# Hybrid DiT trunk: the norms' factors of the time mixing spread by VectorE instead of GpSimd

## The chip, the cores and the metric

The kernel runs on one core of a Trainium2 chip. The metric is the time of one execution on the device in microseconds; the times shown are medians of several runs. A profile comes from one further execution, whose own time stands beside its span.

## The reference

Two layers of a trunk work on 256 context tokens and 256 latent tokens of width 1024. Each layer has an adaLN-modulated RMSNorm, one combined input projection that feeds three token mixers (windowed attention, bidirectional RWKV-7 time mixing, a gated spatial unit), gates that merge them, an output projection, and a dense SwiGLU. The change touches the time mixing alone, at two normalisations over the 64 columns of a head:

```python
kk = heads((k * lp['k_k']).astype(f32))
kk = kk * lax.rsqrt(jnp.sum(kk * kk, -1, keepdims=True) + 1e-12)
...
y = jnp.moveaxis(ys[:, 0] + jnp.flip(ys[:, 1], axis=0), 0, 1)
mu = jnp.mean(y, -1, keepdims=True)
var = jnp.mean(jnp.square(y - mu), -1, keepdims=True)
y = ((y - mu) * lax.rsqrt(var + GN_EPS)).reshape(B, T, C) * lp['ln_w'] + lp['ln_b']
```

The first is the norm of the keys, the second the group norm of the time mixing's output. Layer 0 needs both for all 512 tokens; layer 1, the last, needs the keys for 512 and the output for the 256 latent tokens only.

## The kernel before, in words

Activations lie feature-major: 128 features on the partitions (two heads of 64), tokens along the columns. Products of the projections are made in three passes: weights and activations are split into a high and a low part (`split`, lines 128 to 130: ScalarE casts, VectorE subtracts), and TensorE multiplies high by high, high by low and low by high (`proj`, line 92 through `dm`).

A layer has three stages. `phase_ab` holds the input projections and the three mixers, `phase_m` merges them, `phase_f` is the SwiGLU. In the profiled execution the mixers' stages lie at about 75 to 700 us (layer 0) and 1275 to 1776 us (layer 1).

`phase_ab` is written as a set of generators, one kind for each piece of work: K (`t_common`, keys, values and norm of the keys of one head pair), P (`t_prep`, the decays and scores of one stream), I (`t_inv`, a triangular inverse made on VectorE by lines 645 and 646), C (`t_chain`, the recurrence over chunks, small matmuls of lines 696 to 730, with GpSimd scaling the state in line 709), Q (`t_post`, the group norm and gate of the output), G (the gate projections), T, A and S (attention and the spatial unit, whose gelu has a GpSimd product in line 932). Start times per kind are written by hand in the table `CB` and sorted by `slots` into the order in which the generators are advanced; each kind also has a priority. From this the framework plans the order of the instructions on each engine. Every engine then runs its own list in that order and waits for semaphores.

The norms work as follows. `rnorm` (lines 418 to 430) lets TensorE sum the squares over the columns of each head with a matrix of ones (line 423), so that the sums of 128 tokens stand on the partitions, two heads side by side. `rsqrt` (lines 132 to 142) computes the inverse square root in twelve short VectorE steps (lines 136 to 142) on at most eight columns; its result is `rn`. Lines 428 and 429 spread each factor over 64 columns into the tile `rx`: a product of the repeated factor and a repeated tile of ones, 128x512, or 128x256 for the output norm of layer 1. `rnorm2` (line 436) transposes `rx` on TensorE into PSUM (`knb` for the keys, `gnb` for the output), and VectorE multiplies it onto the keys (line 508) or the output (line 754). `rx` shares a ring of three buffers, `tmp`, with other temporary tiles. There are four head pairs in each layer, each with one norm of the keys and one of the output: 16 calls of `rnorm` in all.

Of the kernel before, what the change touches and what calls it, by code (L numbers as in the profile page):

```python
# [85 lines left out]
def trunk(ctx: ExitStack, tc: tile.TileContext, out, a):  # L86
# [11 lines left out]
    V = nc.vector  # L98
    S = nc.scalar
    G = nc.gpsimd  # L100
# [31 lines left out]
    def rsqrt(pool, out, x, scale, bias, tag):  # L132

        xs = pool.tile(list(out.shape), F32, tag=tag + "x", bufs=1, name="rsx")
        t = pool.tile(list(out.shape), F32, tag=tag + "t", bufs=1, name="rst")
        V.tensor_scalar(xs, x, scale * RS_A, bias * RS_A, op0=ALU.mult, op1=ALU.add)
        V.tensor_scalar(t.bitcast(I32), xs.bitcast(I32), 1, 0x7fffffff, op0=ALU.logical_shift_right, op1=ALU.bitwise_xor)
        V.tensor_scalar(out, t, RS_B, None, op0=ALU.mult)
        for _ in range(3):
            V.tensor_mul(t, out, out)  # L140
            V.scalar_tensor_tensor(t, t, -0.5 / RS_A, xs, op0=ALU.mult, op1=ALU.mult)
            V.scalar_tensor_tensor(out, t, 1.5, out, op0=ALU.add, op1=ALU.mult)
# [234 lines left out]
    def phase_ab(L, extra):  # L377
# [7 lines left out]
        with tc.tile_pool(name="pb", bufs=1, reuse_waits="tile", side="right") as pb, tc.tile_pool(name="pe", bufs=1, reuse_waits="tile") as pe, tc.tile_pool(name="pbp", bufs=1, space=PSUM, reuse_waits="tile") as pbp:  # L385
# [4 lines left out]
            def rc(shape, name):  # L390
                return pbp.tile(shape, F32, tag="rc", bufs=cb["PB"]["rc"], name=name) if "rc" in cb["PB"] else rw(shape, name)
# [4 lines left out]
            def tmc(name, n=512):  # L396
                return pb.tile([128, n], F32, tag="tmc", bufs=cb["BF"]["tmc"], name=name) if "tmc" in cb["BF"] else tmp(name, n)
# [20 lines left out]
            def rnorm(sq, n, scale, bias, name):  # L418

                nt = n // 128  # L420
                pss = rc([128, 4, 2], name + "s")
                for j in range(nt):
                    mm(pss[:, j], sq[:, 128 * j:128 * j + 128], bones[:, 0:128:64], start=True, stop=True)
                rn = pb.tile([128, 4, 2], F32, tag="rn", bufs=2, name="rn")
                rsqrt(pb, rn[:, :nt], pss[:, :nt], scale, bias, "rr")
                rx = tmc("rx")
                rxv = rx[:, :n].rearrange("p (a h d) -> p a h d", h=2, d=64)
                G.tensor_tensor(rxv, rn[:, :nt].unsqueeze(3).broadcast_to([128, nt, 2, 64]),
                                ones[:, 0:64].unsqueeze(1).unsqueeze(1).broadcast_to([128, nt, 2, 64]), op=ALU.mult)
                return rx  # L430

# [42 lines left out]
            def t_common(hp):  # L474
# [26 lines left out]
                sq = tmc("sqk")  # L501
                S.activation(sq, kT, AF.Square, scale=kkc)
                rx = rnorm(sq, 512, 1.0, 1e-12, "kn")
                yield
                rn = rnorm2(rx, 512, "kn")
# [235 lines left out]
            def t_post(hp):  # L741

                need("C", 2 * hp + 1, 99)
                h = H[hp]
                y = h.y
                pm = rc([128, 512], "pm")
                mm(pm[:, :no], bones, y, start=True, stop=True)
                V.scalar_tensor_tensor(y, pm[:, :no], -1.0 / 64, y, op0=ALU.mult, op1=ALU.add)
                sq = tmc("sqy")
                S.activation(sq[:, :no], y, AF.Square)  # L750
                yield
                rx = rnorm(sq, no, 1.0 / 64, 64e-5, "gn")
                yield
                V.tensor_mul(y, y, rnorm2(rx, no, "gn"))
                V.tensor_scalar(y, y, pv[:, V_LW + hp:V_LW + hp + 1], pv[:, V_LB + hp:V_LB + hp + 1], op0=ALU.mult, op1=ALU.add)
                need("K", hp, 99)
                G.tensor_add(y, y, h.bv)
                yield
                pg = rc([128, 512], "pg")
                mm(pg[:, :no], L.gup[:, 128 * hp:128 * hp + 128], sxg, start=True, stop=True)  # L760
                V.tensor_mul(y, y, pg[:, :no])
                G.dma_start(orw_d[:, hp, 256 * so:512], y)
                yield
# [495 lines left out]
```

## Time and profile before

| what | value |
|---|---|
| median of 3 runs | 2076.11 us (2067.94 to 2082.16) |
| profiled execution, its own time | 2055.66 us |
| its span, first to last instruction | 2053.9 us |
| mean granted clock of TensorE | 0.943 |
| busy: TensorE | 1913.0 us |
| busy: VectorE | 1355.0 us |
| busy: ScalarE | 854.5 us |
| busy: GpSimd | 237.7 us |
| instructions | 35061 |

Busy times of the engines lie beside each other and do not add up to the span. A view of waits gives the idle time of an engine ahead of an instruction and the instruction that ended it. The chain that ended last is followed back from the last instruction, at each step to what released it. A granted clock of 1.00 is TensorE's higher level, 2.4 GHz; 0.50 is the lower, 1.2 GHz; a value between them is a mean over a stretch.

### The profile page before, as it was taken

To read this page: it belongs to the slowest core of one execution; us is meant where nothing else is said; L and a number is where in the kernel's file an instruction comes from. 1 tells how busy PE (TensorE), PEld (TensorE's weight loads), DVE (VectorE), ACT (ScalarE), POOL (GpSimd) and SP (SyncE) were. 2 spreads that over 40 slices of the span, in tenths; PEclk is the share of its full clock that TensorE was granted. 3 is DMA by queue.
4 is the path that set the end of the run, shared out by engine and by line. 5 is a ranking of instruction groups with operands and counts; after the bars stand their busy time and mean duration, and the time that the engine had idled before them with its cause. 6 is when DMAs were issued, how large, how long until landed. Compare 5 with 4: busy or idle time off the path is not lost.

```text
span 2053.9 us, 35061 instructions
## 1 busy us (share of the span) xinstructions
PE 1913.0 (93%) x13162; PEld 1527.6 (74%) x13162; DVE 1355.0 (66%) x3657; ACT 854.5 (42%) x1848; POOL 237.7 (12%) x401
## 2 busy tenths in 40 slices
PE   4999989999999989899999997889998999698999
PEld 3877776666666768787887885777776777598999
DVE  4587776477585445688656545696786877476665
ACT  3442333444354433432232334444444555255443
POOL 3111201101001012100000002212020201120000
PEclk8997999989999999999999998988997999599999
DMA  8222213221211585166556422311220222374553
GB/s 286 78 67 79 63 47 114 83 90 53 63 39 55 202 269 163 62 188 212 176 175 212 145 79 76 100 66 32 93 69 14 74 75 88 122 230 146 185 183 105
DMA packets 97094, 239.16 MB, mean 116 GB/s; under 512 B 9594, under 2 KB 25082, under 8 KB 96796
## 3 DMA queue, kind: packets, MB, share of 16 engines
q1 hardware_dynamic: 88860, 223.82, 33.9%
q10 hardware_dynamic: 6912, 9.44, 1.3%
q0 software_dynamic: 1152, 3.67, 0.5%
q8 instruction: 103, 1.69, 0.3%
q14 instruction: 67, 0.55, 0.1%
HBM read 219.59 MB, written 17.30 MB: 115 GB/s over the span
## 4 chain that ended last, share of the span: by engine, by line
PE 74%; DVE 12%; DMA 4%; ACT 4%; issue 4%; POOL 1%; SPq 0%; ACTq 0%; POOLq 0%; DVEq 0%
PE fps L92 17%; PE gps L92 8%; PE rps L92 5%; PE psc L591 3%; PE yps L1094 3%; PE yps L1095 3%; PE yps L1096 3%; DVE wl L130 2%; PE sc L865 2%; DMA mr<-in_w_mod 2%; PE py L701 2%; PE po L893 2%; PE py L730 1%; PE cw L696 1%; PE ops L1026 1%
## 5 line engine op out<-in xcount | busy, mean ns | idle before, releaser
L129 ACT CAST wh<-wr 128x512 fp32r<-128x512 f32 (+1 forms) x560 | 341.7, 614 | 579.2 <-PE fps L92 196.8
L130 DVE TENSOR_TENSOR wl<-wr,wh 128x512 fp32r<-128x512 f32 (+1 forms) x560 | 389.6, 701 | 236.7 <-ACT wh L129 203.7
L92 PE MATMUL fps<-hh,wh 128*128 128x256 f32 (+1 forms) x720 | 241.3, 338 | 2.2 <-ACT hh L351 2.2
L92 PE MATMUL fps<-hh,wl 128*128 128x256 f32 (+1 forms) x720 | 241.6, 336 | 0.0
L92 PE MATMUL fps<-hl,wh 128*128 128x256 f32 (+1 forms) x720 | 240.9, 336 | 0.7 <-POOL hl L356 0.7
L92 PEld LDWEIGHTS fps<-hh,wh 128*128 128x128 f32 x720 | 138.3, 193 | 17.3 <-ACT hh L351 3.0
L92 PEld LDWEIGHTS fps<-hl,wh 128*128 128x128 f32 x720 | 138.3, 193 | 14.0 <-POOL hl L356 1.1
L92 PEld LDWEIGHTS fps<-hh,wl 128*128 128x128 f32 x720 | 138.7, 193 | 12.8
L92 PE MATMUL gps<-hh,wh 128*128 128x512 f32 (+1 forms) x384 | 142.1, 370 | 2.8 <-DVE itp L645 1.4
L92 PE MATMUL gps<-hl,wh 128*128 128x512 f32 (+1 forms) x384 | 140.1, 365 | 0.0
L92 PE MATMUL gps<-hh,wl 128*128 128x512 f32 (+1 forms) x384 | 139.0, 362 | 0.0
L1094 PE MATMUL yps<-fgh,wh 128*128 128x512 f32 (+1 forms) x352 | 118.7, 337 | 0.0
L1096 PE MATMUL yps<-fgh,wl 128*128 128x512 f32 (+1 forms) x352 | 118.3, 336 | 0.0
L1095 PE MATMUL yps<-fgl,wh 128*128 128x512 f32 (+1 forms) x352 | 118.3, 336 | 0.0
L271 DVE SCALAR_TENSOR_TENSOR macc<-mr,cr,macc 128x512 f32<-128x512 f32 x140 | 99.7, 747 | 22.0 <-DMA mr<-in_w_mod 21.4
L645 DVE TENSOR_TENSOR itp<-it,ix 128x60 f32<-128x60 f32 (+24 forms) x496 | 109.1, 222 | 7.1
L646 DVE TENSOR_TENSOR it<-it,itp 128x60 f32<-128x60 f32 (+24 forms) x496 | 108.1, 220 | 7.0
L92 PE MATMUL rps<-hh,wh 128*128 128x512 f32 (+1 forms) x224 | 91.5, 409 | 17.1 <-ACT hh L351 6.4
L92 PE MATMUL rps<-hl,wh 128*128 128x512 f32 (+1 forms) x224 | 91.2, 407 | 0.0
L92 PE MATMUL rps<-hh,wl 128*128 128x512 f32 (+1 forms) x224 | 90.3, 403 | 0.3 <-DVE wl L130 0.3
L92 PEld LDWEIGHTS gps<-hh,wh 128*128 128x128 f32 x384 | 74.6, 194 | 16.3 <-issue 2.6
L591 PE MATMUL psc<-AR,BK 64*128 64x128 f32 (+1 forms) x512 | 80.5, 302 | 6.6 <-DVE SC L592 1.4
(368 smaller groups left out, 4185.3 us busy)
## 6 DMA issues: line engine op xcount, KB each, us to landing
wr<-in_w SPq DMA_DIRECT2D x120, 512.0 KB, 3.5
wr<-in_w_fm SPq DMA_DIRECT2D x84, 512.0 KB, 3.5
mr<-in_w_mod SPq DMA_DIRECT2D x76, 512.0 KB, 4.4
wr<-in_w_o SPq DMA_DIRECT2D x24, 512.0 KB, 4.9
wr<-in_w_tm SPq DMA_DIRECT2D x20, 512.0 KB, 3.4
wr<-in_w_mod SPq DMA_DIRECT2D x20, 512.0 KB, 3.9
wr<-in_w_out SPq DMA_DIRECT2D x16, 512.0 KB, 4.0
gate_d<-gth ACTq DMA_DIRECT2D x24, 256.0 KB, 2.7
```

The lines of the kernel that those rows point to most:

```text
L92: r = mm(*args, **kw)
L129: S.copy(hi, raw)
L130: (eng or V).tensor_sub(lo, raw, hi.bitcast(F32))
L271: V.scalar_tensor_tensor(acc[:, i], w, c[:, i:i + 1], acc[:, i], op0=ALU.mult, op1=ALU.add)
L591: mm(ps[:, c - c0, 0:64 * ns], BK[hs[x], c].rearrange("p a j -> p (a j)"), AR[hs[x], c, 0:ns].rearrange("p a j -> p (a j)"), start=True, s ...
L645: V.tensor_tensor(tv, Tm[:, t0:, s:s + 1].broadcast_to([128, n, s]), X[:, s, 0:s].unsqueeze(1).broadcast_to([128, n, s]), op=ALU.mult)
L646: V.tensor_tensor(Tm[:, t0:, 0:s], Tm[:, t0:, 0:s], tv, op=ALU.add)
L701: mm(py[hs[x], 4 * d + c], VS[hs[x], 4 * d + c, x], AR[hs[x], 4 * d + c, 1], start=False, stop=False)
L865: mm(sc, qT[p0:p0 + 64, pr, qs], kT[p0:p0 + 64, :kn], start=True, stop=qt < 2)
L1094: mm(ps[:, :n], wh, gh_[k][:, :n], start=k == 0, stop=False)
L1095: mm(ps[:, :n], wh, gl_[k][:, :n], start=False, stop=False)
L1096: mm(ps[:, :n], wl, gh_[k][:, :n], start=False, stop=k == nf - 1)
```

## The change

One instruction of `rnorm` goes to VectorE (`V`) where it went to GpSimd (`G`). Its operands, its shape and its result stay as they are, and so does all other code, the table of start times and priorities included.

```diff
                 rx = tmc("rx")
                 rxv = rx[:, :n].rearrange("p (a h d) -> p a h d", h=2, d=64)
-                G.tensor_tensor(rxv, rn[:, :nt].unsqueeze(3).broadcast_to([128, nt, 2, 64]),
+                V.tensor_tensor(rxv, rn[:, :nt].unsqueeze(3).broadcast_to([128, nt, 2, 64]),
                                 ones[:, 0:64].unsqueeze(1).unsqueeze(1).broadcast_to([128, nt, 2, 64]), op=ALU.mult)
                 return rx
```

## Rows read from the trace of the kernel before

**Rows 1.** The page: busy us by engine; shares of the chain that ended last.

```profile
PE 1913.0 (93%) x13162; PEld 1527.6 (74%) x13162; DVE 1355.0 (66%) x3657; ACT 854.5 (42%) x1848; POOL 237.7 (12%) x401
...
PE 74%; DVE 12%; DMA 4%; ACT 4%; issue 4%; POOL 1%; SPq 0%; ACTq 0%; POOLq 0%; DVEq 0%
```

**Rows 2.** Line 428 (ns min/median/max); TensorE's waits for it (us, times, longest).

```profile
L428 POOL TENSOR_TENSOR rx<-rn,ones x16: 613/1044/1519, 116.6 to 1772.7; 128x512 f32<-128x512 f32 x12, 128x256 f32<-128x256 f32 x4
...
PE gnb L436 <- POOL rx L428: 4.3, 3, 3.2
PE knb L436 <- POOL rx L428: 3.6, 5, 1.5
```

**Rows 3.** The chain that ended last, pieces of line 428: start, us.

```profile
116.57 1.06 POOL rx L428
...
1772.70 0.62 POOL rx L428
```

**Rows 4.** Time line around two factors: start us, duration us, engine, line, tiles.

```profile
465.18 0.16 DVE L142 SCALAR_TENSOR_TENSOR rn<-rst,rn 128x8 f32<-128x8 f32 x1
...
465.43 1.05 POOL L428 TENSOR_TENSOR rx<-rn,ones 128x512 f32<-128x512 f32 x1 [23.28 <-DVE st L876]
...
465.48 1.54 DVE L130 TENSOR_TENSOR wl<-wr,wh 128x512 fp32r<-128x512 f32 x1
...
466.53 0.33 PE L436 MATMUL gnb<-cst,rx 128*128 128x128 f32 x1 [0.50 <-POOL rx L428]
...
607.84 1.08 DVE L646 TENSOR_TENSOR it<-it,itp 128x54 f32<-128x54 f32 x1
...
608.95 0.21 DVE L645 TENSOR_TENSOR itp<-it,ix 128x52 f32<-128x52 f32 x1
```

**Rows 5.** Time line at a factor beside which VectorE reads PSUM.

```profile
1505.11 0.61 POOL L428 TENSOR_TENSOR rx<-rn,ones 128x256 f32<-128x256 f32 x1 [3.33 <-DVE rn L142]
1505.17 0.69 DVE L592 TENSOR_TENSOR SC<-psc,cst 128x512 f32<-128x512 f32 x1 [0.20 <-PE psc L591]
```

**Rows 6.** VectorE's groups by form: busy us, mean ns of one, idle before.

```profile
L828 DVE TENSOR_TENSOR qx<-qx,rsq 128x512 f32<-128x512 f32 x6 | 4.1, 685 | 0.1
L507 DVE TENSOR_SCALAR kk<-kT,pv 128x512 f32<-128x512 f32 x8 | 3.9, 483 | 0.0
L837 DVE TENSOR_TENSOR qx<-qx,rcs 128x512 f32<-128x512 f32 x4 | 3.1, 787 | 1.6 <-POOL qb L836 1.6
...
L828 DVE TENSOR_TENSOR qx<-qx,rsq 128x256 f32<-128x256 f32 x4 | 1.7, 418 | 0.0
...
L837 DVE TENSOR_TENSOR qx<-qx,rcs 128x256 f32<-128x256 f32 x2 | 0.8, 424 | 0.4 <-POOL qb L836 0.4
```

**Rows 7.** GpSimd's state products of line 709, ns min/median/max.

```profile
L709 POOL TENSOR_TENSOR csp<-VS,PC x96: 393/401/967, 195.7 to 1758.0; 64x128 f32<-64x128 f32 x96
```

**Rows 8.** VectorE's time line in a stretch of layer 1.

```profile
1521.08 0.16 DVE L141 SCALAR_TENSOR_TENSOR rst<-rst,rsx 128x8 f32<-128x8 f32 x1
1521.19 0.21 DVE L645 TENSOR_TENSOR itp<-it,ix 128x50 f32<-128x50 f32 x1
1521.32 0.16 DVE L142 SCALAR_TENSOR_TENSOR rn<-rst,rn 128x8 f32<-128x8 f32 x1
```

**Rows 9.** Windows in layer 0: busy us, granted clock, DMA share, GB/s.

```profile
125.00:175.00 50.00, 44.88 (x276) 35.57 (x275) 41.77 (x103) 23.28 (x50) 9.54 (x18) 0.83 0.33 102
153.00:158.00 5.00, 3.78 (x49) 2.62 (x46) 4.79 (x18) 2.24 (x5) 1.28 (x1) 1.00 0.51 151
158.00:163.00 5.00, 4.00 (x43) 2.92 (x41) 4.20 (x12) 1.08 (x3) 0.00 (x0) 0.60 0.75 254
163.00:168.00 5.00, 5.00 (x20) 4.33 (x21) 4.14 (x9) 1.71 (x4) 1.50 (x2) 0.50 0.64 179
```

**Rows 10.** Windows of the two mixers' stages; columns PE, PEld, DVE, ACT, POOL.

```profile
75.00:700.00 625.00, 600.32 (x4408) 428.00 (x4407) 418.95 (x1365) 263.93 (x634) 73.42 (x140) 0.96 0.23 72
...
1275.00:1776.00 501.00, 458.85 (x3636) 365.45 (x3635) 371.41 (x1253) 233.09 (x548) 80.10 (x144) 0.89 0.21 67
```

## The prediction

> **What bounds the kernel now.** I read the page first: the busy shares and the chain that ended last. TensorE is busy 93% of the span and holds 74% of the chain, VectorE 66% and 12%, GpSimd 12% and 1% [rows 1]. So an instruction of GpSimd matters only where TensorE stands still for it, and one of VectorE mostly where it sits on that chain.
>
> Second I read the instructions of line 428, who waits for them, and the chain around each of them. The line runs 16 times, on GpSimd, about 1.04 us each for 512 columns [rows 2]. TensorE's matrix queue stood idle for its result in eight of the sixteen, 4.3 + 3.6 = 7.9 us together; 3.2 us of this is one wait at the end of layer 1, which is mostly the wait for the square root ahead of the factor [rows 2]. The chain goes through line 428 seven times, six of them at the long form and the last at the short one; the seven pieces (1.06, 1.04, 1.05, 1.05, 1.53, 1.35 and 0.62 us) sum to 7.70 us, 0.4% of the span [rows 3]. This is the ceiling of what the line itself can give.
>
> Third I read the time line around one of them, for what else it touches. The factor starts 0.09 us after VectorE's last step of the square root ended (465.18 + 0.16 against 465.43), and TensorE starts 0.05 us after it ended. In the same microsecond VectorE's split of a weight tile takes 1.54 us, where other two-operand products of 128x512 take 0.685 [rows 4, 6]. It is the same at 607.84, where a 128x54 product of the inverse takes 1.08 us and the next, 128x52, takes 0.21 [rows 4]. I counted ten of the sixteen in which some VectorE instruction is stretched so, by 0.87 us at most (1.08 - 0.21). Where VectorE was idle, or read one operand from PSUM (0.69 us for 128x512 while line 428 ran), it was not stretched [rows 5]. So today the line costs VectorE time although it does not run there.
>
> **The change, part by part.** *Removed:* 16 GpSimd instructions, 12 of 512 columns and 4 of 256. Nothing else moves: no DMA is issued by this step, and the three queues that issue DMAs lose none. GpSimd has 88% of the span free; what was queued behind the line on it (the chain's state products of line 709, the gelu product of line 932) can only come sooner.
>
> *Added:* the same 16 on VectorE. The nearest row is line 828, also a two-operand product of SBUF tensors with one operand repeated over 64 columns: 0.685 us for 512 columns and 0.418 for 256 [rows 6]. From below I bound it by the one-operand line 507, 0.483 us; from above by line 837, two operands with repeats, 0.787 us [rows 6]. I take line 828, whose operands are nearest. VectorE's load: 12 x 0.685 + 4 x 0.418 = 9.9 us.
>
> *On the path:* seven instances, 6 x 0.685 + 0.418 = 4.53 us in place of 7.70, so -3.2. The crossing from VectorE to GpSimd goes too, 7 x 0.09 = 0.6. The crossing to TensorE stays (VectorE to TensorE in place of GpSimd to TensorE); no row tells their handover times apart, so I take 0, between -0.1 and +0.1 each. Together -3.8 us.
>
> For comparison, the page GPSIMD Engine Reference of the Trainium skill (section 3.1) has a two-input product 1.96 times as long on GpSimd as on VectorE. By that estimate the long form would take 0.53 us and the short one 0.32, and the path would gain 0.9 us more; line 828's rows do not agree with so short a time, and I stay with them.
>
> *VectorE's other work:* it gets 9.9 us more, and loses the stretching, between 0 and 10 x 0.87 = 8.7 us. I take the middle, so +5.5 us net, and as VectorE holds 12% of the chain, +0.7 us. Ends: 0 (it fits into idle time) and +9.9 (every one is late for somebody).
>
> *The wait.* No new semaphore wait is added ahead of the factor on VectorE that holds others up: its input is VectorE's own, and its buffer is one of three that rotate; I found none of the sixteen held by a reader of an old buffer. What is new is that the factor has to take its turn in VectorE's queue, and that a GpSimd instruction may now be the one held: the state product of line 709 takes 0.401 us and once 0.967 [rows 7], so up to 0.57 us each time, at most 16 x 0.57 = 9.1 us and on no chain row seen. I take 0.
>
> The page SBUF — State Buffer of the Trainium skill (Who interferes with whom) speaks against this change there: an instruction of VectorE with two SBUF inputs and one of GpSimd that reads SBUF exclude each other, and the one that issues second waits. By it line 428 would keep the conflict and only turn the loser round. The rows on stretching bear it out; as TensorE waits for little that GpSimd makes, it changes my bound and not my sum.
>
> **Sum:** -3.8 + 0.7 = -3.1 us on the profiled execution's 2055.66 us, or 2052.6. The median of the runs shown, 2076.11, lies 20.5 us above that execution; set on the median the forecast is 2073.0 us. If the order of work stays as it is, the ends are -7.9 (every wait gone) to +11.1 (12 x 0.787 + 4 x 0.424 of VectorE's work, all on the path): 2068 to 2087.
>
> **The rivals.** What can be larger than all this is the order. The rows of VectorE show the steps of one square root (lines 140 to 142), which stand one behind the other in the code, alternating with the inverse (645, 646) [rows 8]: the order on each engine is planned by the framework for engines it thinks busy or free. With 16 steps on another engine the plan from 116 us on may come out otherwise everywhere in the two time-mixing stages. The trace shows one plan only, so I price this by what separates good stretches from bad ones in it: the clock.
>
> *Slower: the new order makes TensorE pause, and its clock falls in layer 0.* Between 153 and 163 us TensorE was busy 3.78 and 4.00 of each 5 us, and the granted clock fell to 0.60 in the second 5 us and to 0.50, the lower of its two levels (1.2 against 2.4 GHz), in the 5 us after, when it was busy without a gap; 125 to 175 us ran at 0.83 on the whole [rows 9]. One such stretch costs 50 x 0.17 = 8.5 us. From three more of them on (25.5 - 3.1 = +22) the kernel is slower by over 1%; three to four give 2098 to 2107 us, 2102 in the middle. For it: layer 0 runs at 0.96 and 96% busy, and has more to lose than to gain. Against: the steps are short, and their plan may heal. Chance 0.23.
>
> *Faster: the new order closes pauses.* The time that the clock took is 625 x 0.04 = 25 us in layer 0's stage and 501 x 0.11 = 55 us in layer 1's [rows 10]. A third of these 80 us with the -3.1 gives -30, or 2046 us; 22% of them is enough for 1%. For it: layer 1's slack and the shorter factor, and the longest of the keys' waits, 1.5 us [rows 2], lies there. Against: nothing in the line's own 7.9 us reaches it. Chance 0.25.
>
> *Hidden in VectorE's queue.* The factor waits for its turn behind splits of 0.69 us and steps of the inverse, where GpSimd took it at once. Half a microsecond each on 16 gives +8 us, or 2081 (within 1%). For it: in stretches the square root's steps already alternate with other work. Chance 0.12, and the forecast itself 0.40.
>
> **How the numbers follow.** A measurement of this kernel can tell about 1%, 21 us, from no change. The forecast and the queue rival lie within it: 0.52. Faster by over 1%: 0.25. Slower: 0.23. The range takes in the likeliest case's 2068 to 2087 and reaches to the middle of both order rivals, 2045 to 2104, which leaves out about a tenth on either side.
>
> **What would show it.** In the changed trace: line 428 on VectorE 16 times at 0.6 to 0.8 us; no wait of TensorE for GpSimd's factor, and waits for VectorE's factor below 7.9 us; splits of 1.5 us beside line 428 gone. If the order was kept, the windows of the two stages have the clocks 0.96 and 0.89 again; if a stage's clock or idle time differs by more than the line's microseconds, an order rival is right. It is wrong if a factor takes over 0.8 us on VectorE, if chains of GpSimd's products grow, or if stages outside time mixing move.

## The result, and the profile after

The changed kernel takes 2045.9 us (median of 4 runs, 2033.94 to 2052.99) against 2077.86 us before (4 runs): 32 us or 1.5% by the medians. The ratio is 0.9861 (95% interval 0.9817 to 0.9906). This ratio and those below leave out runs more than 1.5% above the fastest of the same kernel in the same study; the kernel before has more of those, so its medians lie further off than the ratios say. Timed again with 12 runs it gave 2044.91 us and 0.9895 (0.9856 to 0.9934).

The two profiled executions do not show this difference. After takes 2052.99 us, before took 2055.66, so the pair is 2.7 us apart. Of 91 timed runs of the kernel before (on three chips), 71 were above 2067 us, and its profiled one was among the short ones. What differs between the runs of one kernel is the granted clock: it lay between 0.919 and 0.954 over these 91 runs, 0.932 on the mean, and a line through them falls by 17.3 us for each 0.01 that the clock rises. The profiled execution had 0.943. So I read the local steps from the traces, and the time from the runs with their clocks.

The page after, busy us by engine and shares of the chain (compare [rows 1]):

```profile
PE 1915.4 (93%) x13162; PEld 1526.8 (74%) x13162; DVE 1357.8 (66%) x3673; ACT 854.9 (42%) x1848; POOL 223.3 (11%) x385
...
PE 77%; DVE 11%; DMA 4%; ACT 4%; issue 3%; POOL 1%; SPq 0%; ACTq 0%; DVEq 0%; POOLq 0%
```

VectorE got 16 instructions and 2.8 us (1357.8 against 1355.0), not the 10.5 us that they take: the other 7.7 us are less time in its other instructions. In the trace before, ten of these ran beside GpSimd's factor and took 6.7 us over the median of their form, so most of the 7.7 us fits the stretching that is gone. Line 428 after (ns min/median/max), which answers to [rows 2]:

```profile
L428 DVE TENSOR_TENSOR rx<-rn,ones x16: 414/683/1250, 115.9 to 1769.8; 128x512 f32<-128x512 f32 x12, 128x256 f32<-128x256 f32 x4
```

and its two forms among VectorE's groups (busy us, mean ns of one), beside which [rows 6] stand:

```profile
L428 DVE TENSOR_TENSOR rx<-rn,ones 128x512 f32<-128x512 f32 x12 | 8.8, 732 | 0.2
L428 DVE TENSOR_TENSOR rx<-rn,ones 128x256 f32<-128x256 f32 x4 | 1.7, 422 | 0.1
```

TensorE's waits for it after (us, times, longest) are 4.7 us where they were 7.9 [rows 2], and most of what is left is the wait at the end of layer 1:

```profile
PE gnb L436 <- DVE rx L428: 3.1, 2, 2.9
PE knb L436 <- DVE rx L428: 1.6, 1, 1.6
```

The chain that ended last now holds three pieces of the line (start us, us), 1.75 us together, where it held seven and 7.70 us [rows 3]:

```profile
689.33 0.70 DVE rx L428
...
1529.32 0.61 DVE rx L428
...
1769.82 0.44 DVE rx L428
```

The one factor that took 1.25 us was itself held by GpSimd. In the time line of VectorE and GpSimd after, it issued 0.03 us behind GpSimd's gelu product and ended 0.55 us after it:

```profile
1315.80 0.73 POOL L932 TENSOR_TENSOR gy<-gy,gx 128x256 f32<-128x256 f32 x1 [2.88 <-DVE rn L142]
1315.83 1.25 DVE L428 TENSOR_TENSOR rx<-rn,ones 128x512 f32<-128x512 f32 x1
```

The order changed as well. A line-by-line comparison of TensorE's old list of instructions (8078 rows, repeats in a row counted once) with the new one marks 3258 lines, rows that went and rows that came together, from the first factor on. The windows of the two mixers' stages after (PE, PEld, DVE, ACT, POOL busy, clock) are those of [rows 10] within 0.01 of clock, so this pair of traces cannot tell where 32 us come from, nor, by the clocks alone, that the order changed:

```profile
75.00:700.00 625.00, 603.25 (x4412) 428.35 (x4411) 422.72 (x1377) 267.16 (x640) 66.16 (x132) 0.95 0.23 73
...
1275.00:1776.00 501.00, 459.21 (x3653) 367.03 (x3652) 378.43 (x1269) 235.49 (x553) 75.24 (x138) 0.90 0.21 69
```

### The profile page after: what moved, and what is told of

It is laid out like the page before. It is cut to its first block, busy times and chain, and to the rows that moved or that the text cites. A ratio compares the mean times of both kernels' runs of the same rounds, so it can differ in the third digit from the quotient of the medians.

```text
span 2051.2 us, 35048 instructions
## 1 busy us (share of the span) xinstructions
PE 1915.4 (93%) x13162; PEld 1526.8 (74%) x13162; DVE 1357.8 (66%) x3673; ACT 854.9 (42%) x1848; POOL 223.3 (11%) x385
## 4 chain that ended last, share of the span: by engine, by line
PE 77%; DVE 11%; DMA 4%; ACT 4%; issue 3%; POOL 1%; SPq 0%; ACTq 0%; DVEq 0%; POOLq 0%
PE fps L92 17%; PE gps L92 9%; PE rps L92 6%; PE psc L591 3%; PE yps L1094 3%; PE yps L1095 3%; PE yps L1096 3%; PE py L701 2%; PE sc L865 2%; DVE wl L130 2%; DVE it L646 2%; PE ops L1026 1%; PE py L730 1%; DMA mr<-in_w_mod 1%; PE cu L713 1%
## 5 line engine op out<-in xcount | busy, mean ns | idle before, releaser
L130 DVE TENSOR_TENSOR wl<-wr,wh 128x512 fp32r<-128x512 f32 (+1 forms) x560 | 385.3, 694 | 223.9 <-ACT wh L129 190.8
L92 PEld LDWEIGHTS fps<-hh,wh 128*128 128x128 f32 x720 | 137.8, 192 | 17.3 <-ACT hh L351 3.0
L92 PE MATMUL gps<-hh,wl 128*128 128x512 f32 (+1 forms) x384 | 143.3, 373 | 0.0
```

The lines of the kernel that those rows point to most:

```text
L92: r = mm(*args, **kw)
L130: (eng or V).tensor_sub(lo, raw, hi.bitcast(F32))
```

## The experiments

**How they are read.** Three accounts are held against each other. *Local*: the time is the line's own, about 3 us, and what it stretches. *Engine*: factors on VectorE spare the clock, whatever the order. *Order*: the move makes the framework plan another order, and that order sets the time. What was expected of each run, printed below, calls them theories. For each kernel I give the ratio, the mean granted clock over its timed runs, and the time at the same clock: each run's time moved to 0.945 by the 17.3 us per 0.01 of the kernel before, then the mean, with its standard error. The last estimates what the kernel would take if its clock were the same. The kernel before came to 2054.5, 2054.0 and 2054.5 us on its three chips by this, so kernels timed on different chips can be compared. There are 12 runs of each kernel, but 10 of the nine, and 6 of nudge 1 on VectorE and of the copy; the mean clocks have a standard error of 0.001 to 0.002 (0.003 for nudge 1 on GpSimd). Three runs of 2.6 to 3.0 ms with a mean clock of 0.55 to 0.64, and one whose clock record does not fit its time, are left out of the last two columns. The third column counts lines as above; another way of counting makes the largest about a quarter smaller and keeps the ranking but for close neighbours.

| kernel | factors on VectorE | lines of TensorE's order changed | ratio (95%) | median us | mean clock | us at 0.945 |
|---|---|---|---|---|---|---|
| before (91 runs) | 0 | 0 | 1 | 2076.5 | 0.932 | 2054.4 ± 0.2 |
| changed, again | 16 | 3258 | 0.9895 (0.9856-0.9934) | 2044.9 | 0.9475 | 2046.9 ± 0.5 |
| layer 0 only | 8 | 2000 | 1.0019 (0.9972-1.0066) | 2075.4 | 0.932 | 2050.8 ± 0.5 |
| layer 1 only | 8 | 1258 | 0.9952 (0.9910-0.9994) | 2055.2 | 0.944 | 2052.7 ± 0.9 |
| GpSimd, nudge 1 | 0 | 2165 | 0.9969 (0.9913-1.0026) | 2067.7 | 0.935 | 2048.9 ± 1.0 |
| GpSimd, nudge 2 | 0 | 2317 | 0.9985 (0.9942-1.0027) | 2073.8 | 0.932 | 2052.0 ± 0.3 |
| VectorE, nudge 1 | 16 | 3382 | 0.9863 (0.9814-0.9912) | 2046.0 | 0.9415 | 2039.9 ± 0.9 |
| VectorE, copy | 16 | 2666 | 0.9849 (0.9803-0.9895) | 2044.7 | 0.947 | 2047.0 ± 1.1 |
| GpSimd, twice | 0 | 6253 | 1.0007 (0.9966-1.0048) | 2068.0 | 0.941 | 2061.7 ± 0.7 |
| seven, order kept | 7 | 76 | 0.9988 (0.9942-1.0034) | 2072.6 | 0.9355 | 2053.4 ± 0.8 |
| keys of pair 2, layer 1 | 1 | 1212 | 0.9966 (0.9923-1.0009) | 2067.6 | 0.934 | 2044.8 ± 0.7 |
| output of pair 0, layer 1 | 1 | 1201 | 0.9947 (0.9906-0.9988) | 2066.4 | 0.938 | 2051.3 ± 1.4 |
| the other nine | 9 | 3306 | 0.9934 (0.9900-0.9968) | 2062.8 | 0.938 | 2047.1 ± 1.2 |

**Is it real, and where?** First the changed kernel again, the two halves of the change, and a control that changes only the order.

```diff
-                V.tensor_tensor(rxv, ...
+                (G if l else V).tensor_tensor(rxv, ...      # layer 0 only
+                (V if l else G).tensor_tensor(rxv, ...      # layer 1 only
```
```diff
-    'K': 10, 'P': 34.7   ...  'K': -18.7, 'P': 24.9
+    'K': 10.3, 'P': 34.7 ...  'K': -18.4, 'P': 24.9         # nudge 1, on the kernel before
```

> The changed kernel once more, unaltered, timed beside the kernel before with each run's clock. If the gain is real and the profile of before was merely one of its shorter runs, the ratio is again 0.983 to 0.992 (about 2043 to 2060 against 2077 us). If the local theory is all there is (about 3 us from the line itself), the ratio is 0.998 and the first comparison was a matter of runs; the ratio then lies above 0.994.

> The factor on VectorE in layer 0 only; layer 1 keeps GpSimd. Local theory: three of the seven chain pieces lie in layer 0, so -1.5 us, ratio 0.999. Order theory: layer 0 has the order of the changed kernel, layer 1 one of its own; the time need not lie between the two kernels, and moves by 10 us or more one way or the other. If the gain of 1.4% comes from layer 0's stage, ratio 0.986 to 0.990.

> The factor on VectorE in layer 1 only; layer 0 keeps GpSimd and exactly the order of the kernel before. Local theory: four of the seven chain pieces lie in layer 1, so -2 us, ratio 0.999. Order theory: the stage of layer 1 moves by 10 us or more, layer 0 not at all. If the gain of 1.4% comes from layer 1's stage, ratio 0.986 to 0.990; the two halves together give the whole only if the parts add up.

> The kernel before with GpSimd's factor, and the start time of the key work moved by 0.3 in the hand-written table of both layers: no work is added, removed or moved to another engine, only the planned order changes. Local theory: ratio 1.000 within 0.3%. Order theory: a change of order alone moves the time by as much as the change did, 0.5 to 1.5% one way or the other.

The gain is real: its interval lies below 0.994. At the same clock the changed kernel is 7.5 us below the kernel before (2046.9 against 2054.4); the other 27 us go with the mean clock, 0.9475 against 0.932 (1.55 x 17.3 = 26.8). This is over all runs; over those that the ratio compares the kernel before had 0.9392, and the clock's part is 14 us (0.83 x 17.3). The halves do not add up: by the ratios layer 0 alone gives nothing, layer 1 alone 0.5%, and both together 1.0 to 1.4%. Layer 0 alone, which by the order theory was to move by 10 us or more, moved by 1 us by its median and by 3.6 at the same clock. The nudge, which moves no work, came to 2067.7 us and is not clear of 1 by its ratio, where the order theory asked for 0.5% or more, but it is below by 5.5 ± 1.0 us at the same clock. So at the same clock a new order without any change of engine is worth at least as much as either half of the change (3.6 and 1.7 us).

**Engine or order?** Next, the same nudge on the changed kernel, another way to write the factor on VectorE, a second nudge on GpSimd's, and GpSimd's factor computed twice.

```diff
+                V.tensor_copy(rxv,
+                              rn[:, :nt].unsqueeze(3).broadcast_to([128, nt, 2, 64]))   # copy
```
```diff
-    'Q': 140,  ...  'Q': 99.4
+    'Q': 141,  ...  'Q': 100.4                             # nudge 2, on the kernel before
```
```diff
-                G.tensor_tensor(rxv, ...
+                for _ in range(2): G.tensor_tensor(rxv, ...  # twice
```

> The changed kernel with the start time of the key work moved by 0.3 in the hand-written table, as in the nudged kernel with GpSimd: the factor stays on VectorE, only the planned order changes. So far the two kernels with VectorE's factor in layer 1 had a mean granted clock of 0.9475 and 0.944 over 12 runs each, the three with GpSimd's factor there 0.932 to 0.935. Engine theory (the factor's engine in layer 1 is what spares the clock): mean clock 0.943 or more, ratio 0.985 to 0.993. Order theory (that particular order happened to be good): the clock may come out anywhere between 0.930 and 0.948, and the ratio between 0.990 and 1.003.

> The factor on VectorE as a copy of the repeated factor, with one SBUF operand in place of two (0.48 us for 512 columns by line 507, against 0.685): 2.8 us less work on VectorE, and nothing of it held by GpSimd's reads (0.68 us where the two-operand form took 1.25). Local theory: at the same clock 1 to 3 us below the changed kernel. Engine theory: mean clock 0.943 or more again, ratio 0.983 to 0.992. Order theory: clock anywhere between 0.930 and 0.948.

> The kernel before, GpSimd's factor, with the start time of the output norm's work moved by 1 in the table of both layers. Engine theory: mean clock 0.930 to 0.936, as in the three kernels with GpSimd's factor in layer 1, ratio 0.996 to 1.003. Order theory: clock anywhere between 0.930 and 0.948, ratio 0.988 to 1.006.

> The kernel before with the factor computed twice in a row on GpSimd into the same tile: 15.8 us more of GpSimd's work, each factor 1.04 us (0.61) later, VectorE held for up to 0.87 us more beside ten of them. This doubles the suspected cost without touching VectorE's or TensorE's work. Local theory: at the same granted clock the time is 6 to 9 us above the kernel before, as the change was 7.6 us below it (2046.8 against 2054.4 at 0.945 by lines fitted through the runs). If the factor's time is hidden and the 7.6 us come from the order, it is within 4 us of it at the same clock.

The ratios of the two kernels with all factors on VectorE fell where the engine theory put them, but the nudged one did it with a clock of 0.9415, below the 0.943 that the theory asked for, and with the best time of all at the same clock; its ratio of 0.9863 is below what the order theory allowed (0.990). Nudge 2, which moves no work either, stayed where the engine theory put it, at 0.932 and 0.9985. GpSimd's factor twice had 0.941, on GpSimd: a clock that high does not need the factor on VectorE, and the engine theory's 0.930 to 0.936 for GpSimd's factor is not kept. At the same clock it is 7.3 us above the kernel before, as the local theory asked, but its order is also the one furthest from it, so this is no measure of the line by itself. The copy takes 0.42 us for 512 columns and gains nothing over the product: 2047.0 against 2046.9 us at the same clock. Nor was it free of GpSimd, as I had expected it to be: one copy that issued 0.03 us behind the gelu product of line 932 took 0.99 us.

**The engine with the order kept.** Moved one at a time, seven of the sixteen factors leave the planned order almost alone, and the others change up to 1327 lines of it. So the seven can test the engine, and single ones of the others the order.

```diff
-                G.tensor_tensor(rxv, ...
+                (V if L.v else G).tensor_tensor(rxv, ...
```
```diff
+                L.v = hp in ((0, 3), (0, 1))[l]; rx = rnorm(sq, 512, ..., "kn")   # seven: keys
+                L.v = hp in ((3,), (1, 3))[l]; rx = rnorm(sq, no, ..., "gn")      # seven: outputs
```
The nine are the complement (`not in`); the single ones set it for pair 2's keys or pair 0's output of layer 1 alone.

> Seven of the sixteen factors on VectorE, chosen because moving them leaves the planned order almost as it was (76 of 8078 rows of TensorE's list differ, where the whole change makes 3258): layer 0 the keys of pairs 0 and 3 and the output of pair 3, layer 1 the keys of pairs 0 and 1 and the output of pairs 1 and 3. The engine changes, the order does not. Engine theory (VectorE instead of GpSimd gives the time): 7/16 of the change, ratio 0.993 to 0.996, and a mean clock above 0.937. Order theory: the mean clock stays at the kernel before's 0.929 to 0.935; what is left is the factors' own time, 7/16 of the 7.6 us at the same clock, about -3 us, ratio 0.997 to 1.000.

> One factor of sixteen on VectorE, the keys of pair 2 in layer 1 (1.52 us on GpSimd, the longest wait); 1212 rows of TensorE's list change their place from there on. Engine theory: 1/16 of the change and one long wait, ratio 0.998 to 1.000, mean clock 0.930 to 0.935. Order theory: the stage of layer 1 has another order, so the mean clock leaves 0.930 to 0.935, up or down by 0.005 or more, and the time moves by 8 us or more.

> One factor of sixteen on VectorE, the output of pair 0 in layer 1 (0.61 us on GpSimd, on no chain piece); 1201 rows of TensorE's list change their place. Engine theory: ratio 0.999 to 1.000 and a mean clock of 0.930 to 0.935. Order theory: mean clock off that by 0.005 or more either way, time by 8 us or more.

> The other nine factors on VectorE (those whose move changes the order: 3306 rows of TensorE's list differ), the seven neutral ones on GpSimd as before. Engine theory: 9/16 of the change, ratio 0.992 to 0.995. Order theory: the order is nearly that of the whole change, so the clock's whole gain is there, mean clock 0.943 or more and ratio 0.985 to 0.993; at the same clock about 4 us above the whole change.

Seven factors with the order kept give 1.0 ± 0.8 us at the same clock, and a time that is not told apart from before (0.9988); the mean clock of 0.9355 ± 0.002 lies between what the order theory (up to 0.935) and the engine theory (above 0.937) asked for, and decides nothing. One single factor that no chain piece held, 0.61 us on GpSimd, gives 0.9947 (0.9988 at most, 2.5 us), and the other, 1.52 us on GpSimd, 9.6 us at the same clock. That is more than the factor's own time can give: a new order by itself moves the time.

That it also sets the mean clock is not shown. There the order theory's numbers missed: pair 2's keys left the clock where it was (0.934), pair 0's output came to 0.938 where a step of 0.005 was asked for, and the nine reached only 0.938 and 2062.8 us, a ratio that the engine theory had given for them. By the number of layer 1's factors on VectorE, the mean clock is 0.932 to 0.935 with none (four kernels; GpSimd's factor twice, 0.941, stands out), 0.934 and 0.938 with one, 0.9355 and 0.938 with four, and 0.9415 to 0.9475 with all eight. So an account in which each factor on VectorE spares some clock is still open.

**Where the clock goes.** Most of it is lost in the stage of layer 1. The two mixers' stages (PE, PEld, DVE, ACT, POOL busy, clock) of the kernel with GpSimd's factor and nudge 2, whose profiled execution has a span of 2087.4 us:

```profile
75.00:700.00 625.00, 599.66 (x4420) 428.15 (x4419) 423.08 (x1371) 267.76 (x641) 73.96 (x140) 0.96 0.23 74
1275.00:1776.00 501.00, 468.99 (x3347) 371.98 (x3345) 356.66 (x1199) 221.55 (x521) 75.07 (x136) 0.82 0.19 60
```

From the first to the last matmul of the norms in layer 1, the profiled executions took 449 to 463 us with all eight factors there on VectorE (five executions, clock 0.88 to 0.92), 478 to 480 with one or four of them (four executions, 0.84 to 0.86), 486 to 505 in the two nudges on GpSimd and layer 0 only (0.81 to 0.84), but 467 and 462 in the kernel before and in GpSimd's factor twice (0.89 and 0.90). Each kernel has one such execution, the changed kernel two, and the clock differs between executions of one kernel.

Windows between 1550 and 1650 us, first of the same execution with nudge 2:

```profile
1550.00:1575.00 25.00, 24.06 (x181) 19.12 (x180) 13.67 (x35) 10.00 (x22) 3.10 (x7) 0.68 0.07 25
1575.00:1600.00 25.00, 23.10 (x155) 15.49 (x154) 15.48 (x62) 9.14 (x26) 1.74 (x5) 0.50 0.00 1
1600.00:1625.00 25.00, 21.33 (x110) 17.12 (x108) 14.70 (x61) 9.41 (x21) 1.46 (x3) 0.57 0.12 40
1625.00:1650.00 25.00, 25.00 (x182) 19.19 (x182) 14.93 (x43) 9.27 (x27) 5.98 (x9) 0.68 0.04 14
```

then of the changed kernel:

```profile
1550.00:1575.00 25.00, 23.27 (x216) 17.17 (x215) 18.41 (x63) 13.98 (x38) 3.14 (x6) 0.80 0.07 25
1575.00:1600.00 25.00, 22.44 (x203) 17.98 (x202) 18.77 (x77) 9.87 (x24) 2.43 (x6) 0.73 0.02 4
1600.00:1625.00 25.00, 24.18 (x217) 18.90 (x216) 21.99 (x70) 13.29 (x36) 7.56 (x12) 1.00 0.17 51
1625.00:1650.00 25.00, 24.12 (x169) 19.38 (x167) 22.61 (x77) 14.02 (x27) 2.94 (x7) 1.00 0.32 106
```

In both the clock is already down in the first window (0.68 and 0.80), and TensorE pauses in the second (23.10 and 22.44 us busy of 25). In the changed kernel it is back at 1.00 from 1600 on. In the other it stays between 0.50, the lower level, and 0.68 through all four windows; in the last of them TensorE is busy without a gap, and the clock is 0.68 on the whole. What makes one fall long and the other short these rows do not show: in the second window it is the changed kernel that paused longer. The kernel before's own profile (span 2053.9 us) has the short fall in this place:

```profile
1575.00:1600.00 25.00, 21.05 (x138) 14.85 (x138) 16.37 (x73) 9.73 (x23) 1.01 (x4) 0.72 0.12 40
1600.00:1625.00 25.00, 23.96 (x236) 19.01 (x234) 20.82 (x59) 12.85 (x34) 7.71 (x13) 1.00 0.12 41
```

It has no other profile, so that its longer executions have the long fall there is argued, from three of the five kernels with all of layer 1's factors on GpSimd: over 1550 to 1650 us nudge 1, nudge 2 and layer 0 only had 0.69, 0.61 and 0.61, the kernel before and GpSimd's factor twice 0.87 and 0.83, and those with all on VectorE 0.85 to 0.92.

Nor is it the only place. The stretch ahead of it differs too, here of the nine, then of the changed kernel timed again:

```profile
1275.00:1550.00 275.00, 253.65 (x1723) 206.77 (x1725) 202.37 (x664) 120.97 (x273) 45.80 (x80) 0.86 0.21 67
1275.00:1550.00 275.00, 252.58 (x1923) 203.32 (x1922) 222.41 (x730) 134.59 (x307) 49.08 (x84) 0.94 0.22 70
```

It ran at 0.85 to 0.87 in the two nudges on GpSimd, layer 0 only, both single factors and the nine, and at 0.90 to 0.94 in all others. The nine and pair 0's output, at 0.88 and 0.85 over 1550 to 1650 us, lost their clock here.

## Why the prediction was right and wrong

**The forecast of 2073.0 us missed by 27 us.** The measured 2045.9 us is at the lower edge of the range (2045 to 2104), beyond the likeliest case's own 2068 to 2087. The time is that of the rival that I gave 0.25, the faster order with 2046 us. That the range still holds it, by 0.9 us, is luck: it was cut off at that rival's own middle, and the median of the 12 later runs, 2044.91 us, lies outside.

**The line's own time** is not contradicted. I put the removed chain pieces at -3.8 us and VectorE's load at +0.7, -3.1 together. With the order kept, seven factors gave -1.0 ± 0.8 us at the same clock; scaled to sixteen that is -2.3 ± 1.8, which does not tell -3.1 from nothing.

**The price on VectorE** was near for the instruction (0.683 us median for 0.685) and too high in the net: +2.8 us for the +5.5 I took, since 7.7 us of VectorE's other work went, where I had bounded the stretching by 8.7 us and taken half. The 1.96 of the Trainium skill's page GPSIMD Engine Reference (section 3.1) is for an add of 2048 columns; here the medians of line 428, 12 of its 16 instructions with 512 columns, are 1.044 and 0.683 us, 1.53 times. By my own terms the gain from that estimate was 1.0 us, not 0.9.

**The conflict stayed**, but not only as I bounded it: one factor of 1.25 us behind GpSimd's gelu product, 0.57 us over the median. A factor over 0.8 us was one of my signs of being wrong, and it came true for this one of the sixteen. GpSimd was held too, within my bound: at 1604 us a state product of line 709 that issued 0.11 us behind a factor of 0.42 us took 0.57 us, for a median of 0.40. As a group line 709 did not get longer (399 ns median, 912 at most, for the 401 and 967 of [rows 7]). What the Trainium skill's page SBUF — State Buffer (Who interferes with whom) says of the loser, that the second to issue waits, agrees with both.

```profile
1604.27 0.42 DVE L428 TENSOR_TENSOR rx<-rn,ones 128x256 f32<-128x256 f32 x1
1604.38 0.57 POOL L709 TENSOR_TENSOR csp<-VS,PC 64x128 f32<-64x128 f32 x1
```

**The step that failed is the choice of the likeliest case:** "if the order of work stays as it is". It did not stay, in 3258 lines, and at the same clock orders that move no work differ by 2.4 and 5.5 us from the kernel before, where the engine with the order kept gives 1.0 ± 0.8. The evidence was in my own rows, the alternating steps of [rows 8]. I priced the rival by the clock, a third of the clock's lost time, 27 us, with the line's 3.1; measured it was 26.8 us of clock (14 over the runs that the ratio compares) and 7.5 at the same clock. That the two sizes agree is luck: the third was chosen by no row, the rival's closed pauses are not shown, and the stage clocks it was taken from hardly moved in the profiled pair (0.95 and 0.90 for 0.96 and 0.89), so that by my own sign the order would have been kept. In hindsight its chance was too low, and I set the forecast's base on the median while I took the clock of the stages from a profile of an uncommonly good run (0.943 against a mean of 0.932), so the room to gain was larger than [rows 10] show.

**The slower rival** (a longer fall of the clock in layer 0) was wrong in place: layer 0's stage ran at 0.95 to 0.98 in every trace, layer 1's at 0.82 to 0.91.

**What stays open** is the cause of the larger part, the clock's. The three kernels with all factors on VectorE, in three orders, lie within 2 us of each other by their medians and below all others. One of them differs from the changed kernel in 3913 lines, so this is hardly one lucky order, yet seven factors with the order kept give nearly nothing at the same clock, and no kernel has all sixteen on VectorE in the old order. Whether the planner makes better orders when GpSimd has no part in the norms, or the kernel before merely had a poor one (all twelve others had a lower median, the nearest by 1 us), the runs do not settle. Nor was the long fall of the clock tried by itself: a kernel with the old order and TensorE kept busy there was not run.

## What to carry to other kernels

Where a planner orders the instructions, moving one of them to another engine can be a new order of everything behind it, and the price of that order can exceed the instruction's own: look first whether the lists of the other engines change, and time a control that changes the order and no work. Look at the granted clock of every run before comparing two traces, and compare times at the same clock; one profile of each kernel can hide the whole difference. To test the engine itself, find those instances whose move leaves the order alone.

## What was not expected of the hardware

The same program, run again and again in one study, spread over 3% (2042 to 2102 us in 35 runs on one chip) with the mean granted clock between 0.919 and 0.952, and the time followed the clock by 17.3 us per 0.01. GpSimd's product with two SBUF operands held VectorE's instructions from a 128x512 split to a 128x8 step of 0.17 us, which took 1.05 us beside it, in the profile of the kernel before:

```profile
247.51 1.04 POOL L428 TENSOR_TENSOR rx<-rn,ones 128x512 f32<-128x512 f32 x1 [6.87 <-DVE rsx L136]
247.53 1.05 DVE L137 TENSOR_SCALAR rst<-rsx 128x8 int32<-128x8 int32 x1
```
